# Where a stick-breaking attention and HGRN2 kernel builds its masks, splits its value weights, and lays its first diagonal

## The chip, the cores and the metric

The kernel runs on one core of one Trainium2 chip. The metric is the device time of one execution in microseconds (us); less is better. The engines are named as the profile names them: PE is TensorE (matmuls), DVE is VectorE, ACT is ScalarE, POOL is GpSimd, and SP is the queue from which most loads are issued.

## The reference: what is computed

One layer of a streaming encoder, for one sequence of 1024 tokens of width 1024, in float32:

```python
xn = rmsnorm(x, norm1_g);  u = xn @ w_in
q_sb, k_sb, v_sb, f_raw, i_hg, q_hg, g_hg, gate_sb, gate_hg = split(u)

# 8 heads of 64: strictly causal stick-breaking attention
z = q_sb . k_sb / 8
w = sigmoid(z_ts) * prod over s<j<t of (1 - sigmoid(z_tj));   o_sb = w @ v_sb

# 4 heads of 128: HGRN2 recurrence in chunks
lb = cumsum(softmax(lb_logits));  f = lb + (1 - lb) * sigmoid(f_raw);  k = 1 - f
S_t = diag(f_t) S_(t-1) + k_t v_t^T;   o_t = S_t^T silu(q_hg)_t        # v = i_hg
o_hg = rmsnorm(o_hg) * silu(g_hg)

merged = sigmoid(gate_sb + b) * (o_sb @ w_o_sb) + sigmoid(gate_hg + b) * (o_hg @ w_o_hg)
h = x + merged @ w_out
h = h + relu(rmsnorm(h) @ w_ff1)^2 @ w_ff2;   out = rmsnorm(h, final_g)
```

## The kernel before

**Products.** Every float32 matrix is split into a high and a low half: ACT copies it to the high half (`hi_copy`, L151), DVE subtracts that from the source and writes the low half (`lo_sub`, L156); `hi_lo` (L159) does both. A product is then three matmuls per tile (high by high, high by low, low by high), recorded at L128. A plain product on DVE (`mul`) is recorded at L164. So a matmul that reads a low half waits for DVE, and DVE for ACT.

**Stages, in time.** Norm of x and transposes (to 35 us), the attention heads (35 to 310), the recurrence, head by head (310 to 560), then gates, output product, second norm and MLP. In the attention each item is one head and one block of 128 queries: `scores` (L741) computes z on PE and its sigmoids on ACT, `weights` (L772) runs the reversed product as a scan on DVE (L782) and multiplies (bt by rm, L164), `turn` (L796) transposes the weights on PE (pw, L131) and splits them (wTh, wTl), and `values` (L838) multiplies them with V (po) and adds two halves into osb (L858), which the last one stores (od, by POOL).

**The recurrence.** `hg_levels(h)` (L976) makes the decayed score matrix sc of one head (1024 columns, 8 chunks of 128) from k, q and the decay pp. The diagonal is a sum over channels of k times q: `pairs_of("sd...")` makes the products (sd_x), splits them (sd_h, sd_l), and `sums_of` lets PE sum them with a matrix of ones (sd). Level l then covers blocks of 2 to the l: level 0 and 1 also by such sums (sl_x, sl_h, sl_l, products on DVE, sums on PE), levels 2 to 6 by direct matmuls of k and q (`scores_of`). At each level `mul` folds the decay into k, q and pp for half of the columns at a time; results are laid into sc under masks (`lay`, L1021, and L1077), the diagonal by a product with the identity. The masks are bit patterns of 128 by 128 that `make_masks` (L942) computes from two iotas on POOL and seventeen small operations on DVE; nothing reads them before the recurrence.

**What sets the order.** The program is recorded in one order and a scheduler lays out each engine's queue, which the engine runs strictly in order. `after(a, b)` (L105) makes a stand behind b in the order without a wait. PE's matmuls belong to two lanes: "main" blocks (attention, recurrence) and "fill" steps of a stream of projections `st`; a fill block may run up to AHEAD = 2 main blocks early. `st.advance(n, upto)` issues n fill steps between main blocks; the loop over heads (FILL, L2202 and on) hands out a fixed share of steps to each level. In the stretch concerned the fill is first the projection of head 1's query and gate (pjq, pjg: matmuls of 128x512), then the values of the recurrence for all heads (pji, weights wi).

**Weights of the fill.** `Unit.load` brings raw weights (512 KB each) into one of two buffers tagged "raw" (pool `wts`, bufs=2) and `Unit.split` makes high and low halves. A load waits until the buffer's last reader, normally the low half's subtraction, is done, and the loads of one queue go in order. `Stream._start` splits the unit that begins, and `prefetch` splits the next unit and loads the one behind it. wi is wide: four raw pieces (wir), four splits (wih on ACT, wil on DVE), all recorded at its prefetch.

Of the kernel before, what the change touches and what calls it, by code (L numbers as in the profile page):

```python
# [14 lines left out]
ALU = mybir.AluOpType  # L15
# [10 lines left out]
HGW = 512  # L26
# [13 lines left out]
def kernel(  # L40
# [178 lines left out]
    oml = cpool.tile([P, 4], F32, tag="oml", name="oml")  # L219
    lmx = small.tile([P, 4], F32, tag="lmx", name="lmx")  # L220
    le = small.tile([P, 8], F32, tag="le", name="le")
    def lower_bounds():
        nc.vector.tensor_tensor(
            out=lmx, in0=prm[:, LB0 : LB0 + 4], in1=prm[:, LB1 : LB1 + 4], op=ALU.max
        )
        for j in range(2):
            nc.vector.tensor_tensor(
                out=le[:, 4 * j : 4 * j + 4],
                in0=prm[:, LB0 + 4 * j : LB0 + 4 * j + 4],
                in1=lmx,  # L230
                op=ALU.subtract,
            )
        nc.scalar.activation(le, le, AF.Exp)
        nc.vector.tensor_tensor(out=lmx, in0=le[:, 0:4], in1=le[:, 4:8], op=ALU.add)
        nc.vector.reciprocal(lmx, lmx)
        mul(lb, le[:, 0:4], lmx)
        nc.vector.tensor_scalar(
            out=oml, in0=lb, scalar1=-1.0, scalar2=1.0, op0=ALU.mult, op1=ALU.add
        )

# [531 lines left out]
    def weights(h, qb):  # L772

        nk = (qb + 1) * P
        bt, rm = zs[h, qb]
        cut = qb == NT - 1
        parts = ((512, nk - 1), (0, 512)) if cut else ((0, nk - 1),)
        for i, (a, b) in enumerate(parts):  # L780
            rr = rm[:, a:b][:, ::-1]
            sc = nc.vector.tensor_tensor_scan(  # L782
                out=rr,
                data0=rr,
                data1=bits[:, 1024 - nk + a : 1024 - nk + b][:, ::-1],
                initial=rm[:, b : b + 1] if i else 0.0,
                op0=ALU.mult,
                op1=ALU.max,
            )
            if i == 1 or (qb == 5 and h in (2,)):  # L790
                after(sc, turn_lo[0])
            m = mul(bt[:, a:b], bt[:, a:b], rm[:, a:b])
            if qb == 5:
                after(m, turn_lo[0])
# [83 lines left out]
    def f_epilogue(h):  # L878
# [15 lines left out]

        return ep

    def i_job():
        unit = wide_unit("wi", W_IN, C_I, HGW)

        vs = []  # L900

        def ep(ps, tb):
            for h in range(NHG):
                if tb == 0:
                    vs.append(slot(f"v{h}"))
                    hg[h, "v"] = vs[h]
                nc.scalar.copy(vs[h][:, tb * P : (tb + 1) * P], ps[:, h * P : (h + 1) * P])
            if tb == NT - 1:
                vs.clear()

        return st.add([unit], lambda: token_steps("pji", unit, xn, range(NT), ep, n=HGW))
# [30 lines left out]
    def make_masks():  # L942
        mscr = slot_n("mscr", 4 * P, I32)
        mask_bits = hpool.tile([P, 4 * 512], U8, tag="h", name="masks")
        m_x, m_s, m_gt, m_odd = (mscr[:, i * P : (i + 1) * P] for i in range(4))
        nc.gpsimd.iota(m_x, pattern=[[1, P]], base=0, channel_multiplier=0)
        nc.gpsimd.iota(m_s, pattern=[[0, P]], base=0, channel_multiplier=1)
        nc.vector.tensor_tensor(out=m_gt, in0=m_x, in1=m_s, op=ALU.is_gt)
        nc.vector.tensor_scalar(out=m_odd, in0=m_s, scalar1=1, scalar2=None, op0=ALU.bitwise_and)
        nc.vector.tensor_tensor(out=m_x, in0=m_x, in1=m_s, op=ALU.bitwise_xor)  # L950

        def add_mask(l, m_if):
            nc.vector.tensor_scalar(
                out=m_s, in0=m_x, scalar1=l, scalar2=None, op0=ALU.logical_shift_right
            )
            m = mask_bits[:, len(masks) * P : (len(masks) + 1) * P]
            nc.vector.scalar_tensor_tensor(
                out=m, in0=m_s, scalar=1.0, in1=m_if, op0=ALU.is_equal, op1=ALU.mult
            )
            masks.append(m)  # L960

        for l in (0, *range(2, 5)):
            add_mask(l, m_gt)

        mul(m_odd, m_odd, m_gt)
        add_mask(1, m_odd)
        nc.vector.tensor_tensor(out=m_odd, in0=m_gt, in1=m_odd, op=ALU.subtract)
        add_mask(1, m_odd)
# [7 lines left out]
    def hg_levels(h):  # L976
# [17 lines left out]
        def pairs_of(name, n, *products):  # L994

            t, h_, l_ = (slot_n(f"{name}_{x}", n, d) for x, d in zip("xhl", (F32, F32R, F32R)))
            for (a, b, w), (i, cs) in zip(products, halves()):
                mul(t[:, cs].rearrange("p (n c) -> p n c", c=w) if w else t[:, 0:n], a, b)
            after(hi_lo(h_, l_, t), turn_lo[0] if "sd0" in name else None)
            return name, n, h_, l_  # L1000

        def sums_of(pairs):

            name, n, h_, l_ = pairs
            open_block("main")
            banks = []
            for c0 in range(0, n, 512):
                S = bank(f"{name}_{c0}")
                matmul(S, ones, h_[:, c0 : c0 + 512], start=True, stop=False)
                matmul(S, ones, l_[:, c0 : c0 + 512], start=False, stop=True)  # L1010
                banks.append(S)
            return banks
# [4 lines left out]
        def lay(mask, S, H):  # L1017

            right = sc.rearrange("p (c n two h) -> p c n two h", c=NT, two=2, h=H)[:, :, :, 1]
            m = blocks_of(mask, H)[:, :, 1].unsqueeze(1).to_broadcast([P, NT, P // (2 * H), H])  # L1020
            nc.vector.copy_predicated(  # L1021
                right, m, S.rearrange("p (c n h) -> p c n h", c=NT, h=H)
            )

        pairs = pairs_of(f"sd{h}", T, (k, q, 0))
        for _, cs in halves():
            mul(q[:, cs], q[:, cs], dec[:, cs])
        yield
        for l in range(7):
            H = 1 << l  # L1030
# [4 lines left out]
            if l == 0:  # L1035
                pairs = pairs_of(
                    f"sl{h}_{l}", 512, (blocks_of(k, 1)[:, :, 0, 0], blocks_of(q, 1)[:, :, 1, 0], 0)
                )
            elif l == 1:
                kv, qv = blocks_of(k, 2)[:, :, 0], blocks_of(q, 2)[:, :, 1]  # L1040
                pairs = pairs_of(
                    f"sl{h}_{l}",
                    T,
                    *((kv[:, :, i : i + 1].to_broadcast([P, T // 4, 2]), qv, 2) for i in (1, 0)),
                )
            elif l < 5:
                banks = scores_of(f"sl{h}_{l}")
            else:
                open_block("main")
                S = bank(f"sl{h}_{l}")  # L1050
                for i, s0 in enumerate(c * P + b for c in range(NT) for b in blocks):
                    matmul(
                        S[0:H, i * H : (i + 1) * H],
                        k[:, s0 : s0 + H],
                        q[:, s0 + H : s0 + 2 * H],
                        start=True,
                        stop=True,
                    )
# [4 lines left out]
                mul(qv[:, :, 1, :], qv[:, :, 1, :], left.to_broadcast([P, n, H]))  # L1063
                hg_level[0] = mul(right, right, left)
            if l == 0:
                for i, cs in halves():
                    mul(chunks(sc[:, cs]), chunks(sums[i]), over_chunks(ident))
            elif l == 1:
                lay(masks[0], sums[0], 1)
            elif l == 2:  # L1070
                for m, S in zip(masks[-2:], sums):
                    lay(m, S, 2)
# [1084 lines left out]
    turns["on"] = False  # L2157
    turn_vectors(1, 6)
    lower_bounds()
    st.advance(11, j_qk[0])  # L2160
    scores(*items[0])
    weights(*items[0])
    st.advance(1, j_qk[0])
    scores(*items[1])
    make_masks()
    st.finish(j_qk[0])

    n_fill = 9 * (j_q[1] - j_qk[0]) + 9
# [4 lines left out]
    for i, it in enumerate(items):  # L2173
        if i + 1 < len(items):
            weights(*items[i + 1])
        if i + 2 < len(items):
            st.finish(j_qk[items[min(i + 4, len(items) - 1)][0]])
            scores(*items[i + 2])
        if i % 2 == 1:
            next(wsums, None)  # L2180
        want = n_first + (i + 1) * (n_fill - n_first) // len(items)
        st.advance(want - done, j_q[1])
        done = want
        before = ready.popleft() if ready else None

        def between():
            if before:
                values(*before)

        r = turn(*it, between)  # L2190
        if i == len(items) - 2:
            attended[0] = turn_lo[0]
        if it[1] != NT - 1:
            between()
        if r:
            ready.append(r)
    while ready:
        values(*ready.popleft())
    st.finish(j_q[1])


    FILL = (3.75, 3.3, 2.7, 2.5, 2.9)  # L2202
# [120 lines left out]
```

## Time and profile before

| | us |
|---|---|
| time, median of 3 runs | 1444.68 (1444.64 to 1444.85) |
| the profiled execution | 1444.55 |
| its span, first to last instruction | 1442.8 |
| PE busy | 1430.3 (99%) |
| DVE busy | 1105.2 (77%) |
| ACT busy | 665.4 (46%) |
| POOL busy | 141.0 (10%) |
| mean granted TensorE clock | 0.999 of full speed |

A row of the timeline reads: start and duration in us, engine, line, operation, destination from sources, shapes, number of instructions in the row; in brackets the idle time of the engine before it and what released it. Instructions of one engine overlap a little, as the next starts before the last has ended, so distances between starts say more than durations. A row of the waits reads: engine, what it was about to write and the line, what it waited for, then us in total, how often, and the longest. A row of stretches reads: from and to, length, then busy us and instructions of PE, PE's weight loads, DVE, ACT and POOL, the granted clock, the share of the DMA engines and their GB/s. A row of one tile reads: line, engine, operation, count, then duration in ns (least, median, most) and first and last start in us; and the landing times of its transfers from issue.

### The profile page before, as it was taken

The page shows a single profiled execution, that of the slowest core. Times are in us where ns is not written, and L with a number is a line of the kernel's source. Part 1 is how long each engine was busy: PE and PEld are TensorE (multiplying, and loading weights), DVE is VectorE, ACT ScalarE, POOL GpSimd, SP SyncE. Part 2 cuts the span into 40 slices and gives each one's busy share as a digit, 9 for nine tenths or more (in the row PEclk, how much of TensorE's full clock was granted, in tenths as well). Part 3 has the DMA queues.
Part 4 walks back from the last instruction along what each step waited for, and adds up shares of the span by engine and source line. Part 5 has one row for each costly group of instructions (what it writes and reads, how often), then busy time and mean ns, then how long its engine had stood idle before and what let it go on. Part 6 is the DMA issues. An engine that isn't in the chain of part 4 may idle for free.

```text
span 1442.8 us, 19614 instructions
## 1 busy us (share of the span) xinstructions
PE 1430.3 (99%) x7272; PEld 1209.7 (84%) x7272; DVE 1105.2 (77%) x1583; ACT 665.4 (46%) x1151; POOL 141.0 (10%) x338
## 2 busy tenths in 40 slices
PE   9999999999999999999999999999999999999998
PEld 8889988888888888888888888888888888888886
DVE  7799898988367798788787898666666757768765
ACT  7566666652223244432335574444444433523343
POOL 3121122200000012100000300000000000000042
PEclk9999999999999999999999999999999999999999
DMA  7135154341113349755487415344445974776825
GB/s 213 48 92 130 32 108 76 73 99 42 52 45 102 88 153 254 240 178 171 142 298 250 155 50 182 130 143 159 155 151 206 354 262 170 261 276 233 288 100 184
DMA packets 157751, 228.85 MB, mean 159 GB/s; under 512 B 25772, under 2 KB 91864, under 8 KB 157656
## 3 DMA queue, kind: packets, MB, share of 16 engines
q1 hardware_dynamic: 142680, 186.96, 38.5%
q0 software_dynamic: 11520, 34.61, 9.2%
q10 hardware_dynamic: 3456, 6.03, 1.1%
q8 instruction: 57, 0.93, 0.3%
q14 instruction: 38, 0.31, 0.1%
HBM read 164.12 MB, written 63.44 MB: 158 GB/s over the span
## 4 chain that ended last, share of the span: by engine, by line
PE 94%; DVE 2%; ACT 1%; issue 1%; DMA 1%; POOL 1%; SPq 0%; DVEq 0%; ACTq 0%; POOLq 0%
PE pm L128 21%; PE pX L128 9%; PE pW L128 6%; PE pY L128 6%; PE pjqk L128 5%; PE pga L128 3%; PE pjq L128 3%; PE pjf L128 3%; PE pys L128 3%; PE pyh L128 3%; PE gY L128 3%; PE gX L128 3%; PE pji L128 3%; PE po L128 3%; PE sl L128 2%; PE pjg L128 2%
## 5 line engine op out<-in xcount | busy, mean ns | idle before, releaser
L151 ACT CAST whid<-w 128x1024 fp32r<-128x1024 f32 x30 | 31.6, 1054 | 154.1 <-PE pm L128 89.4
L782 DVE TENSOR_TENSOR_SCAN rm<-rm,bits 128x511 f32<-128x511 f32 (+7 forms) x72 | 87.3, 1219 | 13.5 <-ACT rm L760 13.4
L128 PE MATMUL pm<-wlod,sh 128*128 128x512 f32 x240 | 93.5, 389 | 0.0
L128 PE MATMUL pm<-whid,sl 128*128 128x512 f32 x240 | 93.4, 389 | 0.0
L128 PE MATMUL pm<-whid,sh 128*128 128x512 f32 x240 | 93.4, 389 | 0.0
L128 PE MATMUL pm<-tl,sh 128*128 128x512 f32 (+1 forms) x210 | 81.3, 387 | 0.0
L128 PE MATMUL pm<-th,sl 128*128 128x512 f32 (+1 forms) x210 | 81.3, 387 | 0.0
L128 PE MATMUL pm<-th,sh 128*128 128x512 f32 (+1 forms) x210 | 81.3, 387 | 0.0
L156 DVE TENSOR_TENSOR wlod<-w,whid 128x1024 fp32r<-128x1024 f32 x30 | 36.6, 1221 | 55.2 <-ACT whid L151 55.2
L156 DVE TENSOR_TENSOR sl<-sa,sh 128x1024 fp32r<-128x1024 f32 x56 | 68.2, 1217 | 0.3 <-ACT sh L151 0.3
L151 ACT CAST wTh<-pw 128x512 fp32r<-128x512 f32 (+2 forms) x96 | 44.0, 486 | 51.3 <-PE pw L131 50.7
L151 ACT CAST sh<-sa 128x1024 fp32r<-128x1024 f32 x56 | 57.2, 1046 | 7.4 <-DMA sa<-ad 7.4
L1963 POOL TENSOR_SCALAR fss<-fss 128x1 f32<-128x1 f32 x8 | 4.5, 561 | 562.1 <-ACT fsc L1958 561.6
L128 PEld LDWEIGHTS pm<-wlod,sh 128*128 128x128 f32 x240 | 45.0, 188 | 9.8 <-DVE wlod L156 0.4
L128 PEld LDWEIGHTS pm<-whid,sl 128*128 128x128 f32 x240 | 45.1, 188 | 9.3
L128 PEld LDWEIGHTS pm<-whid,sh 128*128 128x128 f32 x240 | 45.0, 187 | 9.3
L156 DVE TENSOR_TENSOR wTl<-pw,wTh 128x512 fp32r<-128x512 f32 (+2 forms) x96 | 50.6, 547 | 2.8 <-ACT wTh L151 2.1
L164 DVE TENSOR_TENSOR bt<-bt,rm 128x511 f32<-128x511 f32 (+7 forms) x72 | 49.0, 685 | 3.6
L128 PE MATMUL pX<-sql,t1h 128*128 128x512 f32 x128 | 50.0, 391 | 0.1
L128 PE MATMUL pX<-sqh,t1l 128*128 128x512 f32 x128 | 49.8, 389 | 0.0
L128 PE MATMUL pX<-sqh,t1h 128*128 128x512 f32 x128 | 49.8, 389 | 0.0
L760 ACT ACTIVATE rm<-z 128x511 f32<-128x511 f32 (+4 forms) x96 | 48.1, 502 | 3.1 <-PE z L128 1.2
(921 smaller groups left out, 4520.8 us busy)
## 6 DMA issues: line engine op xcount, KB each, us to landing
w<-in_w_ff_dram SPq DMA_DIRECT2D x72, 512.0 KB, 5.1
sa<-ad SPq DMA_DIRECT2D x56, 512.0 KB, 6.8
ad<-a SPq DMA_DIRECT2D x32, 256.0 KB, 2.1
ad<-s SPq DMA_DIRECT2D x16, 512.0 KB, 5.8
tw<-in_w_out_dram POOLq DMA_DIRECT2D x24, 256.0 KB, 3.9
x<-in_x_dram SPq DMA_DIRECT2D x8, 512.0 KB, 8.6
xnl<-xnh POOLq DMA_DIRECT2D x8, 512.0 KB, 11.0
pr<-pd SPq DMA_DIRECT2D x8, 512.0 KB, 6.4
```

Source lines behind the costliest of these rows:

```text
L128: return pe(nc.tensor.matmul(*a, **k))
L151: hi_last[0] = after(in_turn("act", nc.scalar.copy(dst, src)), hi_behind[0])
L156: nc.vector.tensor_tensor(out=dst, in0=src, in1=hi.bitcast(F32), op=ALU.subtract),
L164: return nc.vector.tensor_tensor(out=out, in0=a, in1=b, op=ALU.mult)
L760: nc.scalar.activation(rm[:, s0 + c0 - 1 : s0 + m - 1], z[:, c0:m], AF.Sigmoid, scale=-0.125)
L782: sc = nc.vector.tensor_tensor_scan(out=rr, data0=rr, data1=bits[:, 1024 - nk + a : 1024 - nk + b][:, ::-1], initial=rm[:, b : b + 1] if i ...
L1963: nc.gpsimd.tensor_scalar(out=ssq, in0=ssq, scalar1=1.0 / D, scalar2=EPS, op0=ALU.mult, op1=ALU.add)
```

## The change

Four things change; the numbers of instructions stay.

1. `make_masks()` is called right after `lower_bounds()` instead of after the second `scores`. Its first two DVE operations stand behind the last of `lower_bounds` (`bounded`, L237), and the scan of the first attention item stands behind the last mask (`masked`).
2. The unit wi becomes a `ByParts` unit: the prefetch only records the loads of the four raw pieces; the four splits are recorded one at a time in `hg_levels(0)`: after the first products q by decay, after level 0's products, and ahead of and behind level 1's.
3. In `pairs_of` the order "behind the last attention weights' split" for head 0's diagonal (`turn_lo`) moves from the split to the product sd_x. The products q by decay stand behind sd_x. The diagonal of head 0 is laid one level later, behind the products of level 1 (`pairs[4]`), and the copy of level 0's sums stands behind the remainder sl_l of level 1 (`pairs[5]`).
4. One fill step is issued ahead of the last `values`, and `st.finish(j_q[1])` moves in front of them.

```diff
--- before.py
+++ after.py
@@ -219,6 +219,8 @@
     oml = cpool.tile([P, 4], F32, tag="oml", name="oml")
     lmx = small.tile([P, 4], F32, tag="lmx", name="lmx")
     le = small.tile([P, 8], F32, tag="le", name="le")
+    bounded, masked = [None], [None]
+
     def lower_bounds():
         nc.vector.tensor_tensor(
             out=lmx, in0=prm[:, LB0 : LB0 + 4], in1=prm[:, LB1 : LB1 + 4], op=ALU.max
@@ -234,7 +236,7 @@
         nc.vector.tensor_tensor(out=lmx, in0=le[:, 0:4], in1=le[:, 4:8], op=ALU.add)
         nc.vector.reciprocal(lmx, lmx)
         mul(lb, le[:, 0:4], lmx)
-        nc.vector.tensor_scalar(
+        bounded[0] = nc.vector.tensor_scalar(
             out=oml, in0=lb, scalar1=-1.0, scalar2=1.0, op0=ALU.mult, op1=ALU.add
         )
 
@@ -787,6 +789,8 @@
                 op0=ALU.mult,
                 op1=ALU.max,
             )
+            if (h, qb) == items[0]:
+                after(sc, masked[0])
             if i == 1 or (qb == 5 and h in (2,)):
                 after(sc, turn_lo[0])
             m = mul(bt[:, a:b], bt[:, a:b], rm[:, a:b])
@@ -894,8 +898,19 @@
 
         return ep
 
+    class ByParts(Unit):
+        def split(self, upto=None):
+            self.load()
+            if self.hl is None:
+                self.hl = []
+            else:
+                Unit.split(self, upto)
+
+    u_i = wide_unit("wi", W_IN, C_I, HGW)
+    u_i.__class__ = ByParts
+
     def i_job():
-        unit = wide_unit("wi", W_IN, C_I, HGW)
+        unit = u_i
 
         vs = []
 
@@ -945,8 +960,8 @@
         m_x, m_s, m_gt, m_odd = (mscr[:, i * P : (i + 1) * P] for i in range(4))
         nc.gpsimd.iota(m_x, pattern=[[1, P]], base=0, channel_multiplier=0)
         nc.gpsimd.iota(m_s, pattern=[[0, P]], base=0, channel_multiplier=1)
-        nc.vector.tensor_tensor(out=m_gt, in0=m_x, in1=m_s, op=ALU.is_gt)
-        nc.vector.tensor_scalar(out=m_odd, in0=m_s, scalar1=1, scalar2=None, op0=ALU.bitwise_and)
+        after(nc.vector.tensor_tensor(out=m_gt, in0=m_x, in1=m_s, op=ALU.is_gt), bounded[0])
+        after(nc.vector.tensor_scalar(out=m_odd, in0=m_s, scalar1=1, scalar2=None, op0=ALU.bitwise_and), bounded[0])
         nc.vector.tensor_tensor(out=m_x, in0=m_x, in1=m_s, op=ALU.bitwise_xor)
 
         def add_mask(l, m_if):
@@ -954,10 +969,11 @@
                 out=m_s, in0=m_x, scalar1=l, scalar2=None, op0=ALU.logical_shift_right
             )
             m = mask_bits[:, len(masks) * P : (len(masks) + 1) * P]
-            nc.vector.scalar_tensor_tensor(
+            made = nc.vector.scalar_tensor_tensor(
                 out=m, in0=m_s, scalar=1.0, in1=m_if, op0=ALU.is_equal, op1=ALU.mult
             )
             masks.append(m)
+            masked[0] = made
 
         for l in (0, *range(2, 5)):
             add_mask(l, m_gt)
@@ -995,13 +1011,13 @@
 
             t, h_, l_ = (slot_n(f"{name}_{x}", n, d) for x, d in zip("xhl", (F32, F32R, F32R)))
             for (a, b, w), (i, cs) in zip(products, halves()):
-                mul(t[:, cs].rearrange("p (n c) -> p n c", c=w) if w else t[:, 0:n], a, b)
-            after(hi_lo(h_, l_, t), turn_lo[0] if "sd0" in name else None)
-            return name, n, h_, l_
+                x = mul(t[:, cs].rearrange("p (n c) -> p n c", c=w) if w else t[:, 0:n], a, b)
+                after(x, turn_lo[0] if "sd0" in name else None)
+            return name, n, h_, l_, x, hi_lo(h_, l_, t)
 
         def sums_of(pairs):
 
-            name, n, h_, l_ = pairs
+            name, n, h_, l_ = pairs[:4]
             open_block("main")
             banks = []
             for c0 in range(0, n, 512):
@@ -1018,13 +1034,19 @@
 
             right = sc.rearrange("p (c n two h) -> p c n two h", c=NT, two=2, h=H)[:, :, :, 1]
             m = blocks_of(mask, H)[:, :, 1].unsqueeze(1).to_broadcast([P, NT, P // (2 * H), H])
-            nc.vector.copy_predicated(
+            return nc.vector.copy_predicated(
                 right, m, S.rearrange("p (c n h) -> p c n h", c=NT, h=H)
             )
+
+        def diagonal(sums, behind=None):
+            for i, cs in halves():
+                after(mul(chunks(sc[:, cs]), chunks(sums[i]), over_chunks(ident)), behind)
 
         pairs = pairs_of(f"sd{h}", T, (k, q, 0))
         for _, cs in halves():
-            mul(q[:, cs], q[:, cs], dec[:, cs])
+            after(mul(q[:, cs], q[:, cs], dec[:, cs]), pairs[4])
+        if h == 0:
+            u_i.split(1)
         yield
         for l in range(7):
             H = 1 << l
@@ -1036,13 +1058,19 @@
                 pairs = pairs_of(
                     f"sl{h}_{l}", 512, (blocks_of(k, 1)[:, :, 0, 0], blocks_of(q, 1)[:, :, 1, 0], 0)
                 )
+                if h == 0:
+                    u_i.split(2)
             elif l == 1:
+                if h == 0:
+                    u_i.split(3)
                 kv, qv = blocks_of(k, 2)[:, :, 0], blocks_of(q, 2)[:, :, 1]
                 pairs = pairs_of(
                     f"sl{h}_{l}",
                     T,
                     *((kv[:, :, i : i + 1].to_broadcast([P, T // 4, 2]), qv, 2) for i in (1, 0)),
                 )
+                if h == 0:
+                    u_i.split()
             elif l < 5:
                 banks = scores_of(f"sl{h}_{l}")
             else:
@@ -1063,10 +1091,14 @@
                 mul(qv[:, :, 1, :], qv[:, :, 1, :], left.to_broadcast([P, n, H]))
                 hg_level[0] = mul(right, right, left)
             if l == 0:
-                for i, cs in halves():
-                    mul(chunks(sc[:, cs]), chunks(sums[i]), over_chunks(ident))
+                if h > 0:
+                    diagonal(sums)
+                else:
+                    first_sums = sums
             elif l == 1:
-                lay(masks[0], sums[0], 1)
+                if h == 0:
+                    diagonal(first_sums, pairs[4])
+                after(lay(masks[0], sums[0], 1), pairs[5] if h == 0 else None)
             elif l == 2:
                 for m, S in zip(masks[-2:], sums):
                     lay(m, S, 2)
@@ -2157,12 +2189,12 @@
     turns["on"] = False
     turn_vectors(1, 6)
     lower_bounds()
+    make_masks()
     st.advance(11, j_qk[0])
     scores(*items[0])
     weights(*items[0])
     st.advance(1, j_qk[0])
     scores(*items[1])
-    make_masks()
     st.finish(j_qk[0])
 
     n_fill = 9 * (j_q[1] - j_qk[0]) + 9
@@ -2194,9 +2226,10 @@
             between()
         if r:
             ready.append(r)
+    st.finish(j_q[1])
+    st.advance(1, j_hg[1])
     while ready:
         values(*ready.popleft())
-    st.finish(j_q[1])
 
 
     FILL = (3.75, 3.3, 2.7, 2.5, 2.9)
```

In the queues that the scheduler makes of it, PE runs four of the six matmuls of that fill step (pjg) between the first and second po of the last values, and one fill step more stands ahead of each main block of head 0; from head 1's diagonal on, the order on PE is as before. DVE's order differs in the two stretches concerned, and the two iotas on POOL come behind the memset of ones at the start. The order of the loads on SP is unchanged.

## The prediction

> **What bounds the kernel now.** I read the busy shares first, then TensorE's waits, then the instructions around each wait.
>
> ```profile
> PE 1430.3 (99%) x7272; PEld 1209.7 (84%) x7272; DVE 1105.2 (77%) x1583; ACT 665.4 (46%) x1151; POOL 141.0 (10%) x338
> ```
>
> TensorE (PE) is busy for 1430.3 of the 1442.8 us span. The change adds and removes no matmul, so all it can win is time in which PE waits.
>
> ```profile
> engine line waited for: us in total, times, longest us
> PE warm L128 <- POOL ident masks.py:199: 2.2, 1, 2.2
> PE po L128 <- DVE wTl L156: 1.5, 2, 1.0
> PE sl L128 <- DVE sl_l L156: 1.0, 1, 1.0
> ```
>
> The 2.2 us is the start of the program, before anything can be multiplied, and stays. The two po waits and the sl wait are the prize. Each is for the low half of a split (L156), which VectorE (DVE) makes.
>
> ```profile
> 68.22 0.36 PE L128 MATMUL po<-wTh,V 128*128 128x256 f32 x1
> 69.61 0.39 PE L128 MATMUL po<-wTl,V 128*128 128x256 f32 x1 [1.02 <-DVE wTl L156]
> 69.83 0.28 PE L128 MATMUL po<-wTh,V 128*128 128x256 f32 x1
> 69.95 0.29 PE L128 MATMUL po<-wTl,V 128*128 128x256 f32 x1
> ...
> 309.45 0.38 PE L128 MATMUL po<-wTh,V 128*128 128x256 f32 x1 [0.18 <-ACT wTh L151]
> 310.30 0.39 PE L128 MATMUL po<-wTl,V 128*128 128x256 f32 x1 [0.47 <-DVE wTl L156]
> 310.52 0.28 PE L128 MATMUL po<-wTh,V 128*128 128x256 f32 x1
> ...
> 327.66 0.39 PE L128 MATMUL sl<-sl_h,ones 128*128 128x512 f32 x1
> 329.06 0.50 PE L128 MATMUL sl<-sl_l,ones 128*128 128x512 f32 x1 [1.01 <-DVE sl_l L156]
> 329.40 0.40 PE L128 MATMUL sl<-sl_h,ones 128*128 128x512 f32 x1
> ...
> 329.87 1.95 PE L128 MATMUL sl<-q,k 128*128 128x128 f32 x16
> 331.57 0.48 PE L128 MATMUL pji<-wih,xnh 128*128 128x512 f32 x1
> ```
>
> The bracketed idle time starts at a matmul's modelled end, so I measure the loss from start to start. Undisturbed po matmuls start 0.12 us apart (69.83 to 69.95), wide ones 0.23–0.24 (two from 329.40 to 329.87). First place: 69.61 − 68.22 − 0.12 = 1.27 us, and the next start comes 0.22 instead of 0.12 later: 1.37. Second: 310.30 − 309.45 − 0.12 = 0.73, plus 0.10: 0.83. Third: 329.06 − 327.66 − 0.23 = 1.17, plus 0.34 − 0.23 = 0.11: 1.28. Together **3.48 us**. That is the ceiling, and about 0.24% of the time.
>
> **The change part by part.**
>
> *Masks behind the lower bounds.* What makes wTl late at the first place:
>
> ```profile
> 67.03 0.28 DVE L957 SCALAR_TENSOR_TENSOR masks<-mscr 128x128 uint8<-128x128 int32 x1
> 67.23 1.74 DVE L782 TENSOR_TENSOR_SCAN rm<-rm,bits 128x767 f32<-128x767 f32 x1
> 68.90 1.12 DVE L156 TENSOR_TENSOR wTl<-pw,wTh 128x512 fp32r<-128x512 f32 x2
> L957 DVE SCALAR_TENSOR_TENSOR masks<-mscr 128x128 uint8<-128x128 int32 x6 | 1.6, 270 | 0.0
> L953 DVE TENSOR_SCALAR mscr<-mscr 128x128 int32<-128x128 int32 x6 | 1.3, 219 | 0.0
> 66.55 0.96 ACT L151 CAST wTh<-pw 128x512 fp32r<-128x512 f32 x2
> ```
>
> Twelve of the mask operations, six of L957 and six of L953, are 2.9 us busy between 56.5 and 67.3, and five more are like them; as the next instruction can start some 0.2 us after such a one (67.03 to 67.23), less after the short L953, all seventeen cost DVE about 3 us. All stand ahead of the 1.74 us scan, and the scan ahead of wTl. Without them the scan ends about 3 us earlier, near 65.9. ScalarE's (ACT) wTh then decides: its two pieces take 0.48 each from 66.55, so the first wTl runs from about 67.1 to 67.8. PE wants it at 68.22 + 0.12 = 68.34: 0.5 us to spare. The whole 1.37 goes.
>
> The masks move here:
>
> ```profile
> 38.98 0.17 DVE L237 TENSOR_SCALAR oml<-lb 128x4 f32<-128x4 f32 x1
> 41.51 0.69 DVE L156 TENSOR_TENSOR KS<-pjqk,KS 64x512 fp32r<-64x512 f32 x1 [2.36 <-ACT QH L151]
> ```
>
> DVE is idle for 2.36 us behind oml, and the scheduler lays twelve of the mask operations ahead of KS and five among its followers. If they run over, KS and QL slip by up to 0.7 us (3 less 2.36); what they feed, a transfer of QL and then z, is not among PE's waits today, so it has some room that I can't size from a row. Price 0, at worst 0.7. The two POOL iotas (0.27 us each) go behind the memset of ones, where POOL next waits for x; price 0.
>
> *One fill step ahead of the last values.* One step of six pjg matmuls now comes before head 0's recurrence, and four of the six are issued between the first and the second po of the second place. 4 × 0.23 = 0.9 us of work that was due anyway stands where PE lost 0.73, so the 0.83 goes. The 0.18 us on wTh in front stays. Their weights were split long before:
>
> ```profile
> L156 DVE TENSOR_TENSOR wg1l<-wg1r,wg1h x1: 1199/1199/1199, 292.7 to 292.7; 128x1024 fp32r<-128x1024 f32 x1
> ```
>
>  The price is passed on: every main block of head 0 now has one fill step more in front, and the next block needing DVE is met later by PE, which helps.
>
> *Value weights one by one, remainders first.* The third place:
>
> ```profile
> 313.33 2.56 SPq L136 DMA_DIRECT2D wir<-in_w_in_dram  x2
> 314.50 0.58 POOL L867 DMA_DIRECT2D od<-osb  x1 [13.10 <-DVE osb L858]
> 321.70 1.23 DVE L156 TENSOR_TENSOR wil<-wir,wih 128x1024 fp32r<-128x1024 f32 x1 [1.59 <-ACT wih L151]
> 322.96 1.29 DVE L164 TENSOR_TENSOR sc<-sd,ident 128x512 f32<-128x512 f32 x2
> 324.16 0.68 DVE L164 TENSOR_TENSOR g<-pjg,g 128x512 f32<-128x512 f32 x1
> 324.76 1.28 DVE L164 TENSOR_TENSOR sl_x<-k,q 128x512 f32<-128x512 f32 x2
> 325.96 1.32 DVE L1021 COPY_PREDICATED sc<-masks,sl 128x512 f32<-128x512 uint8 x1
> 327.78 1.22 DVE L156 TENSOR_TENSOR sl_l<-sl_x,sl_h 128x1024 fp32r<-128x1024 f32 x1
> DMA to landing us min/median/max: 3.7/4.4/5.0
> ```
>
> DVE stood 1.59 us at the fourth wil, whose raw weights were issued at 315.5 (the second of two SP issues that end at 315.89) and took 5.0; behind it came the diagonal (sc, 1.2 us), g, the products sl_x, the copy of the level-0 sums (1.1 us) and two small ones, then sl_l. In the new order DVE does sd_x, osb, q, osb, sd_l, wil, sl_x, wil, sl_l, six small k/q/pp steps, g, and then the third wil, which I call S. Adding start-to-start distances (1.13 for a 1024 split or product, 0.6 for 512, 0.33 for k or q) from the wTl at 309.56, with the second osb waiting for the last po until about 314.1, puts its earliest start at S = 321.9. Then come sl_x (1.2), five small steps (1.67) and sl_l (1.13): the remainder is ready at S + 5.25 = 327.2. PE reaches sl_1 at 327.66 − 0.83 (second place) + 6 × 0.227 (one fill step more in front) = 328.2 and its sl_l at 328.4. Over 1 us to spare; the 1.28 goes. The 18 pji matmuls in front of it start at 324.1, and the third wil, for the last six, is needed at 326.8 and done at 323.1.
>
> What is late next: the work that was put back. It fills a DVE already full:
>
> ```profile
> 321.70:342.80 21.10, 20.09 (x105) 16.88 (x105) 21.07 (x38) 6.17 (x14) 0.00 (x0) 1.00 0.31 89
> ...
> 331.91 1.22 DVE L1187 TENSOR_TENSOR wga0r<-wga0r,wga0r 128x1024 f32<-128x1024 f32 x1
> 335.45 0.42 DVE L164 TENSOR_TENSOR q<-q,pp 128x256 f32<-128x256 f32 x1
> 342.34 0.42 DVE L164 TENSOR_TENSOR q<-q,pp 128x256 f32<-128x256 f32 x1
> ```
>
> DVE (the third pair of numbers) is busy 21.07 of 21.10 us from the fourth wil to the last q that level 4 needs, which ends at 342.76, 21.06 after that wil. The new order has in that stretch one wil more (+1.14), one g less (−0.60) and one q of head 1 less (−0.64): 20.96 from S, so 342.9 for S = 321.9. PE goes from 328.2 through sl_1 (0.9), level 2 (329.87 to 331.57: 1.7), 24 pji (5.45), level 3 (1.7) and 18 pji (4.1) to level 4's first half at about 342.2 and its second 0.85 later, at 343.05; q for the first half is ready at S + 20.2 = 342.1. For level 3 the last q (335.45 + 0.42 is 14.17 behind the old wil) is ready at S + 14.7 = 336.6, against 337.2. So level 4 has 0.1–0.2 us to spare, level 3 0.5. The subtraction on wga0r stands at S + 10.75 = 332.6; its load can only be issued when the fourth wil frees the raw buffer, about S + 6.45 = 328.4, and took
>
> ```profile
> DMA to landing us min/median/max: 4.5/4.5/4.5
> ```
>
> so it lands near 332.9, 0.2 late. I put 0.2 us for these against the sum. Any delay of S beyond 321.9 comes out at PE nearly one for one.
>
> What can delay S is the third raw load. Two buffers serve four loads, and now it waits for the first wil (315.6 to 316.9) instead of being issued at 313.33. Landing plus ACT's wih (1.05) must come by 321.9, so it may take 4.0 us. Of the rows 3.7, 4.4 and 5.0, I take 3.7: the 5.0 load was issued 1.0 us behind the 512 KB od store (314.50) and while the load before it was in flight; in the new order no other load is, and the store, issued with the last osb near 314.6, is 2.3 us ahead. With 4.4, S is 0.5 later and the sum 2.8; with 5.0, 1.1 later and 2.2. The Trainium skill ("DMA: Bandwidth & Descriptors", "Anatomy of one DMA — SWDGE (gpsimd) path") gives about 2.0 us fixed plus bytes at 436 GB/s: for 512 KB an estimate of 3.2 us, by which S would not move and the sum stay as it is. This trace's rows are 0.5 to 1.8 us above that, and they decide.
>
> **Sum.** 1.37 + 0.83 + 1.28 − 0.2 = 3.3 us. The profiled execution took 1444.55 (span 1442.77 and 1.8 around it), the median of the runs is 1444.68, 0.13 more: 1444.68 − 3.3 = **1441.4 us**. What a measurement of this kernel tells from no change is about 0.2%, or 2.89 us; faster means below 1441.79.
>
> **The rivals.**
>
> *The wait moves to levels 3 and 4.* The third wir takes 4.4 to 5.0 or DVE loses as much elsewhere. For it: DVE has no idle time there to absorb anything. Against: the slower load shared its time with the store. The gain is 2.2 to 2.8 (1441.9 to 1442.5), centre 1442.2, inside 0.2%.
>
> *One place isn't cured.* If wTl stays behind some other work at the first place, 1.37 stays: 1442.7. If sl_l does (an ACT cast of wih ahead of sl_h), 1.28 stays: 1442.6. Against: margins of 0.5 and 1.2 us. The masks could also push QL into the next z; that would cost at most 0.7.
>
> *Slower: the raw loads run late.* The one serial chain that became longer is wil, buffer free, load, wih, wil, buffer free, wga0r load. At 3.7 us it costs nothing; beyond 4.0 each us costs one, the gain of 3.3 is used up at 4.0 + 3.3 = 7.3 us, and slower by over 0.2% needs 10.2. The rows reach 5.0 here; a load of 7.5 gives 1444.9. A wait of more than 3.4 us would by the Trainium skill ("TensorE: Matmul & The Clock Gate", "What's actually happening") also halve the clock for a while; the granted clock around today's waits of 1.0 us is 1.00, and no run here shows more.
>
> **How the numbers follow.** Forecast 0.62; the wait moves 0.20; one place isn't cured 0.10; slower chain 0.08, most of it for what I haven't seen in a schedule this dense. Only the forecast is faster by over 0.2%, and close to the bound; the middle cases give 0.31 within 0.2%, as does a little of the last; 0.07 slower. The low end is the ceiling, 1444.68 − 3.48, less 0.2 for the spread: 1441.0. The high end takes in the moved wait and the uncured places, 1442.9; this leaves out about one in ten. The forecast's own range is 1441.0 to 1441.8.
>
> **What would show it.** PE's waits keep no po on wTl above 0.1 us and no sl on sl_l; the scan of 767 starts near 64.2; DVE runs masks from 39.2. At 320 to 330 (all later times shifted by about 1.4 us earlier) DVE starts its third wil without a wait on ACT. Wrong would be: a new PE wait at sl<-q,k near 335 to 342 (the chain of waits then names DVE q, before it wga0r or wih and a DMA), po still waiting near 68, or loads of wir above 4.0 us.

## The result, and the profile after

The changed kernel takes 1441.95 us (median of 14 runs, 1441.26 to 1442.30) against 1444.68 (14 runs, 1444.31 to 1445.03): 2.73 us less, a ratio of 0.998 with a 95% interval of 0.9972 to 0.9988. The forecast was 1441.4 with a range of 1441.0 to 1442.9. The gain is real, though just under the 0.2% (2.89 us) that the chances were drawn by; the median lies with the first rival (1441.9 to 1442.5), where the wait moves to level 4.

The profiled execution took 1442.05 with a span of 1440.2, 2.6 less than before. Its waits of TensorE, columns as before:

```profile
PE warm L128 <- POOL ident masks.py:199: 2.2, 1, 2.2
PE pjqk L128 <- DVE xnl L334: 0.3, 1, 0.3
PE po L128 <- ACT wTh L151: 0.2, 1, 0.2
PE pjv L128 <- ACT wv0h L151: 0.2, 1, 0.2
PE sl L128 <- DVE q L164: 0.2, 1, 0.2
```

The two po waits on wTl and the sl wait on sl_l are gone. Two small ones are new: pjv near 14 us, and sl on q, which is level 4 of head 0. PE at the three places, and at level 4 (timeline of the changed kernel):

```profile
68.65 0.36 PE L128 MATMUL po<-wTh,V 128*128 128x256 f32 x1
68.85 0.28 PE L128 MATMUL po<-wTl,V 128*128 128x256 f32 x1
...
308.59 0.39 PE L128 MATMUL po<-wTh,V 128*128 128x256 f32 x1 [0.18 <-ACT wTh L151]
308.81 0.40 PE L128 MATMUL pjg<-xnh,wg1h 128*128 128x512 f32 x1
...
309.51 0.40 PE L128 MATMUL pjg<-xnh,wg1h 128*128 128x512 f32 x1
309.75 0.27 PE L128 MATMUL po<-wTl,V 128*128 128x256 f32 x1
...
327.44 0.39 PE L128 MATMUL sl<-sl_h,ones 128*128 128x512 f32 x1
327.67 0.39 PE L128 MATMUL sl<-sl_l,ones 128*128 128x512 f32 x1
...
341.90 1.27 PE L128 MATMUL sl<-q,k 128*128 128x128 f32 x9 [0.16 <-DVE q L164]
```

At the first place the po on wTl now follows the one on wTh by 0.20 instead of 1.39; at the second, four pjg stand between them; at the third, sl_l follows sl_h at the undisturbed 0.23. At level 4 the first matmul starts 0.32 late and the next one 0.11 more: 0.43 us lost.

DVE in the stretch of the masks and at the third wil:

```profile
39.37 0.17 DVE L239 TENSOR_SCALAR oml<-lb 128x4 f32<-128x4 f32 x1
39.45 0.28 DVE L963 TENSOR_TENSOR mscr<-mscr 128x128 int32<-128x128 int32 x1
...
42.54 0.69 DVE L156 TENSOR_TENSOR KS<-pjqk,KS 64x512 fp32r<-64x512 f32 x1
...
64.75 1.74 DVE L784 TENSOR_TENSOR_SCAN rm<-rm,bits 128x767 f32<-128x767 f32 x1
67.58 1.15 DVE L156 TENSOR_TENSOR wTl<-pw,wTh 128x512 fp32r<-128x512 f32 x2 [1.09 <-ACT wTh L151]
...
321.66 1.23 DVE L156 TENSOR_TENSOR wil<-wir,wih 128x1024 fp32r<-128x1024 f32 x1 [0.36 <-ACT wih L151]
...
342.22 0.42 DVE L164 TENSOR_TENSOR q<-q,pp 128x256 f32<-128x256 f32 x1
```

The scan of 767 runs 2.5 us earlier, although this profile is 0.4 us late at this point, and wTl now waits for ACT. The third wil waited 0.36 for ACT's wih. Whether that wait is what comes out at level 4 is tested below. ACT and SP show where it comes from:

```profile
316.26 2.11 SPq L136 DMA_DIRECT2D wir<-in_w_in_dram  x2
320.57 1.05 ACT L151 CAST wih<-wir 128x1024 fp32r<-128x1024 f32 x1 [2.54 <-DMA wir<-in_w_in_dram]
```

The load was issued at 316.26 and used at 320.57: 4.3 us, 4.2 of them to its landing, where the forecast had 4.0 as the limit.

### The profile page after: what moved, and what is told of

Same layout as the page of the kernel before. It is cut to its first block, busy times and chain, and to the rows that moved or that the text cites. A ratio compares the mean times of both kernels' runs of the same rounds, so it can differ in the third digit from the quotient of the medians.

```text
span 1440.2 us, 19612 instructions
## 1 busy us (share of the span) xinstructions
PE 1430.0 (99%) x7272; PEld 1210.0 (84%) x7272; DVE 1106.4 (77%) x1583; ACT 665.7 (46%) x1151; POOL 137.8 (10%) x338
## 4 chain that ended last, share of the span: by engine, by line
PE 95%; DVE 2%; DMA 1%; issue 1%; POOL 1%; ACT 1%; SPq 0%; DVEq 0%; POOLq 0%; ACTq 0%
PE pm L128 21%; PE pX L128 9%; PE pW L128 6%; PE pY L128 6%; PE pjqk L128 6%; PE pga L128 3%; PE pjq L128 3%; PE pjf L128 3%; PE pys L128 3%; PE pyh L128 3%; PE gY L128 3%; PE gX L128 3%; PE po L128 3%; PE z L128 2%; PE pjv L128 2%; PE pjg L128 2%
```

## The experiments

The runs come in three groups of four, each measured beside the kernel before. That took 1444.70 in the first group (the load early, head 1's sd_x late, both, the iotas late), 1444.63 in the second (the load early with the gate's split kept, the masks alone, wi split whole, the old order of the diagonal) and 1445.07 in the third (the fill step alone, the masks undone, and two repeats). As these differ by 0.44, a difference of less than half a us between groups says little by itself.

**The wait at level 4: the load, or DVE's amount of work?** Two edits of the changed kernel relieve either.

```diff
+    u_i.roomy = (2,)       # the third raw piece of wi gets a slot of its own
```

> The changed kernel with the third raw piece of wi loaded into a slot of its own, so that it waits for no split. The changed kernel took 1441.95 (median), with DVE idle for 0.36 us at the third wil and PE losing 0.43 us at level 4 of head 0 (start to start). Theory: the late load put those 0.36 us into a full DVE queue, and they came out at level 4. Then the wait at the third wil goes, the loss at level 4 falls by 0.36 or all of it, and the time is about 1441.55 (1441.4 to 1441.7). Rival: DVE's amount of work alone makes level 4 late; then the loss at level 4 stays above 0.3 and the time at 1441.9 to 1442.0.

1441.91 (1441.77 to 1442.55): no gain. The wait at the third wil and the loss at level 4 were gone, but PE's waits had a new line, and the timeline shows where:

```profile
PE sl L128 <- DVE sc L164: 0.5, 1, 0.5
327.97 1.05 PE L128 MATMUL sl<-q,k 128*128 128x128 f32 x8
329.51 1.16 PE L128 MATMUL sl<-q,k 128*128 128x128 f32 x8 [0.48 <-DVE sc L164]
...
323.38 1.23 DVE L156 TENSOR_TENSOR wga0wlo<-wga0r,wga0whi 128x1024 fp32r<-128x1024 f32 x1
...
328.76 1.29 DVE L164 TENSOR_TENSOR sc<-sd,ident 128x512 f32<-128x512 f32 x2
```

With the load early, the scheduler had also moved the split of the gate's weights (wga0wlo) ahead of sl_l, from 331 to 323. That pushed the diagonal (sc) back, and the second half of level 2 waits for it (sl behind sc: the diagonal still holds the PSUM bank). Level 2's sixteen matmuls took 2.45 us from first start to next instead of 1.70: 0.75 us lost. So neither theory was tested cleanly; what it did show is that laying the diagonal one level later leaves its banks little to spare.

```diff
@@ pairs_of
-                after(x, turn_lo[0] if "sd0" in name else None)
+                after(x, turn_lo[0] if "sd0" in name else level3[0] if "sd1" in name else None)
@@ behind the k, q, pp steps of level 3
+            if h == 0 and l == 3:
+                level3[0] = hg_level[0]
```

> The changed kernel with head 1's products sd_x (one DVE instruction, 1.2 us) put behind the k, q and pp steps that level 4 of head 0 needs. Theory (a full DVE queue sets level 4): the loss of 0.43 us at level 4 goes though the load stays late and the wait at the third wil stays 0.3 to 0.4; time about 1441.5. Rival: the moved product is late for its own sums on PE (head 1's sd) and the loss comes back there; 1441.9 or more.

1441.38 (1440.96 to 1441.86), with no loss at level 4. That is the time the theory gave. Its other half, a wait of 0.3 to 0.4 us at the third wil, did not come: the third load happened to land earlier, and its wil started at 321.01, 0.65 earlier than in the changed kernel's profile, after an idle time of 0.05. So this run doesn't decide.

```diff
@@ both edits
+    u_i.roomy = (2,)
+                after(x, turn_lo[0] if "sd0" in name else level3[0] if "sd1" in name else None)
```

> The third raw piece of wi early and head 1's sd_x late, together. If both act on the same loss at level 4 (0.43 us), the two together give what each gives alone, about 1441.5, with no loss above 0.1 at level 4. If they act on different losses, more: 1441.1.

1442.00 (1441.44 to 1442.57): the moved gate split was there again and PE lost 0.67 at level 2, so this says the same as the first run.

To take the load alone, the gate's split was tied back to its place:

```diff
+    u_i.roomy = (2,)
@@ RawUnit.split, first gate unit
-            hi_lo(h, l, ra)
+            lo = hi_lo(h, l, ra)
+            if self.name == "wga0":
+                after(lo, laid0[0])     # behind the copy of level 0's sums
```

> The changed kernel with the third raw piece of wi in a slot of its own, as in the run before, but with the split of the gate's weights (wga0) kept behind the copy of level 0's sums, so that DVE's order is that of the changed kernel. In the run before, this split had moved ahead of sl_l, and PE lost 0.65 us at level 2, where a PSUM bank is held by the diagonal's product sc. Theory: in the old order both losses are gone, at level 2 and at level 4: 1441.45 (1441.3 to 1441.7), the third wil starts without a wait. Rival: the early load itself does the harm; 1441.9.

1441.34 (1441.13 to 1441.98). The loss at level 2 and the late start of level 4 are gone, with the wil at

```profile
321.11 1.22 DVE L156 TENSOR_TENSOR wil<-wir,wih 128x1024 fp32r<-128x1024 f32 x1
```

and no wait; 0.10 us stays behind the first matmul of level 4. The changed kernel was not in this group, but of its 25 runs elsewhere 11 took more than 1442.0, and of these 11 none. The profiles in which DVE's order in this stretch is the changed kernel's and the load is late say the same (us):

| profile | third load, issue to landing | DVE idle before the third wil | lost at level 4 |
|---|---|---|---|
| changed kernel | 4.2 | 0.36 | 0.43 |
| iotas late | 4.0 | 0.15 | 0.33 |
| masks undone | 4.0 | 0.11 | 0.32 |
| changed kernel, second profile | 3.8 | 0 | 0.12 |

So both theories hold a part: about 0.1 us is lost even when DVE doesn't wait, as its queue is full, and the rest goes with the late load. When the load isn't late, the forecast's figure of 1441.4 is reached.

**Is the start late because of the iotas?**

```diff
-        nc.gpsimd.iota(m_x, pattern=[[1, P]], base=0, channel_multiplier=0)
-        nc.gpsimd.iota(m_s, pattern=[[0, P]], base=0, channel_multiplier=1)
+        after(nc.gpsimd.iota(m_x, ...), last_power[0])
+        after(nc.gpsimd.iota(m_s, ...), last_power[0])
```

> The changed kernel with the two iotas on POOL behind the norms' last power, instead of behind the memset of ones at 2.3 us. In the profiles the changed kernel's PE is 0.37 us later than the kernel before at 18 us, because the second raw value weight landed later (ACT waits for it until 13.28). Theory A: this is chance in the first loads, not the iotas: time 1441.95 within 0.2, runs spread from 1441.3 to 1442.3 as in the changed kernel. Theory B: the iotas disturb the first loads: the start is as before, time about 1441.55, and the runs lie close together.

1441.71 (1441.32 to 1441.93), between the two theories. But the run with the early third load and the changed kernel's own second profile have the iotas in the same early place, and there PE starts pjv 0.34 and 0.17 us earlier than in the first profile, without that wait. So the iotas don't make it late by themselves; that it is chance in the first loads is the reading left, which no run shows, and the runs' spread isn't settled by it.

**The parts alone.**

```diff
@@ the kernel before, with the masks' move alone (and the two orders that hold them there)
+    make_masks()            # behind lower_bounds()
-    make_masks()            # behind the second scores
```

> The kernel before with the masks' move alone (order behind the lower bounds, first scan behind the last mask). Theory: the wait of po on wTl near 69 goes and nothing else changes: 1444.68 - 1.37 = 1443.3, and the waits near 310 and 329 stay at 0.5 and 1.0 us. Rival: DVE's time in front (12 masks ahead of KS) is paid at z; 1443.6 or more.

1443.94 (1443.10 to 1444.33): 0.7 us, half of what was expected. The profile is of the slowest of these runs. Near 69 the loss is gone, and PE is 1.25 us ahead. But:

```profile
PE sl L128 <- DVE sl_l L156: 1.3, 1, 1.3
PE po L128 <- DVE wTl L156: 0.5, 1, 0.5
PE sl L128 <- DVE q L164: 0.4, 1, 0.4
...
311.97 2.55 SPq L136 DMA_DIRECT2D wir<-in_w_in_dram  x2
320.83 1.23 DVE L156 TENSOR_TENSOR wil<-wir,wih 128x1024 fp32r<-128x1024 f32 x1 [1.84 <-ACT wih L151]
```

the wait for sl_l grew from 1.0 to 1.3 (1.56 instead of 1.17 from start to start), because ACT could cast the last raw piece only 0.87 us earlier than before (319.75 instead of 320.62), and the end of head 3's levels near 556 took 0.66 us longer. In this profile other places gave most of the gain back; how much they do in a median run is not shown. Undoing the masks from the changed kernel gives the other side:

```diff
@@ the changed kernel, with the masks as before
-    make_masks()            # behind lower_bounds()
+    make_masks()            # behind the second scores
```

> The changed kernel with the masks built where they were. Alone, the masks' move gave 0.7 instead of 1.37, as the wait for sl_l grew by 0.4 and loads near 555 were late in its profile. Theory: place by place the masks are worth 1.37 us: 1441.9 + 1.37 = 1443.3. Rival: they are worth 0.7: 1442.6.

1443.07 (1442.77 to 1443.85) against 1441.90 of the changed kernel in the same group: the masks are worth 1.17, with 1.26 us lost again at po near 69.6. Where the later waits are out of the way, the masks bring nearly what the first place lost.

```diff
@@ the kernel before, with the fill step alone
+    st.finish(j_q[1])
+    st.advance(1, j_hg[1])
     while ready:
         values(*ready.popleft())
-    st.finish(j_q[1])
```

> The kernel before with the fill step ahead of the last values alone. The step begins the unit whose prefetch splits wi, so all four wil are recorded, and laid by the scheduler, ahead of sd_x. Theory: the loss of 0.83 us near 310 goes and about 6 us come at head 0's diagonal, with the TensorE clock lower for some us behind so long a wait, as without the splitting by parts (1449.4): 1450 (1448.5 to 1452). Rival: the step alone gives its 0.8: 1443.9.

1450.94 (1450.58 to 1451.43), 5.9 us slower than before. And the changed kernel without the splitting by parts:

```diff
-    u_i.__class__ = ByParts
```

> The changed kernel with wi split whole at its prefetch, all else as changed. The prefetch is recorded at the fill step, which now lies ahead of the last values, so that all four wil stand ahead of sd_x on DVE, two of them behind loads that wait for buffers. Theory: sd_x comes near 321 and sd_l near 323.5 to 324, where PE wants it at 317.5; PE loses about 6 us: 1448 (1446 to 1450), slower than before. Rival: the splits one by one are a refinement worth the 1.28 us at level 1 at most; 1442 to 1443.3.

1449.37 (1447.80 to 1450.68). In both, head 0's diagonal waits 5.9 us. PE and DVE of the second:

```profile
315.94 0.39 PE L128 MATMUL pjg<-xnh,wg1l 128*128 128x512 f32 x1
322.26 1.22 PE L128 MATMUL sd<-sd_h,ones 128*128 128x512 f32 x2 [5.93 <-ACT sd_h L151]
...
309.71 2.35 DVE L156 TENSOR_TENSOR wil<-wir,wih 128x1024 fp32r<-128x1024 f32 x2
312.09 0.99 DVE L862 TENSOR_TENSOR osb<-po,ot 64x256 f32<-64x256 f32 x2
315.91 1.23 DVE L156 TENSOR_TENSOR wil<-wir,wih 128x1024 fp32r<-128x1024 f32 x1 [2.83 <-ACT wih L151]
318.71 1.23 DVE L156 TENSOR_TENSOR wil<-wir,wih 128x1024 fp32r<-128x1024 f32 x1 [1.58 <-ACT wih L151]
319.85 1.22 DVE L164 TENSOR_TENSOR sd_x<-k,q 128x1024 f32<-128x1024 f32 x1
322.31 1.22 DVE L156 TENSOR_TENSOR sd_l<-sd_x,sd_h 128x1024 fp32r<-128x1024 f32 x1
```

The fill step begins its unit, and with it the prefetch: the four splits of wi come ahead of sd_x in DVE's queue, the last two waiting 2.83 and 1.58 us for loads. So the splitting by parts is first of all what makes the fill step possible.

The loss is larger than the wait. Stretches of the same profile, columns as before, and two of its matmuls:

```profile
310.00:316.00 6.00, 6.00 (x35) 5.17 (x34) 3.01 (x5) 1.78 (x3) 0.58 (x1) 1.00 0.59 191
322.00:328.00 6.00, 5.74 (x13) 4.30 (x14) 5.97 (x13) 2.27 (x4) 0.00 (x0) 0.50 0.20 58
328.60:334.00 5.40, 5.40 (x25) 4.41 (x25) 5.40 (x11) 1.65 (x2) 0.00 (x0) 1.00 0.00 0
327.17 0.63 PE L128 MATMUL pjg<-xnl,wg1h 128*128 128x512 f32 x1
327.59 0.63 PE L128 MATMUL pjg<-xnh,wg1l 128*128 128x512 f32 x1
```

Behind the wait the granted clock is 0.50 for some 6 us, and matmuls start 0.42 apart instead of 0.23; of the 9.1 us lost from 316 to 328.4, 6.1 are the wait and 3.0 the clock. That agrees with what the Trainium skill says ("TensorE: Matmul & The Clock Gate", "What's actually happening"), that an idle window of about 3.4 us puts TensorE to half its clock. In the run with the fill step alone less was enough: the clock fell 2.4 us after the last matmul's end (317.7 to 320.2), and the measurement decides. The waits of 1.0 us before the change lay in stretches with a clock of 1.00.

The run with the fill step alone waited as long (5.87 us) and lost less. The clock is 0.50 for some 6.8 us in both profiles, but with the fill step alone from 320.2 to 327.0, and without the splitting by parts from 321.5 to 328.4. The first stretch lies half within the wait: only 3.4 us of it were left when PE went on, and 1.7 us were lost to it instead of 3.0. So the price of such a wait depends also on when the clock falls.

The splitting by parts alone, and the changed kernel without the fill step, were not run; what these two are worth is read from the profile.

**Is the new order of the diagonal needed?** The changed kernel without its third part:

```diff
-                after(x, turn_lo[0] if "sd0" in name else None)
-            return name, n, h_, l_, x, hi_lo(h_, l_, t)
+            return name, n, h_, l_, x, after(hi_lo(h_, l_, t), turn_lo[0] if "sd0" in name else None)
-            after(mul(q[:, cs], q[:, cs], dec[:, cs]), pairs[4])
+            mul(q[:, cs], q[:, cs], dec[:, cs])
-                if h > 0:
-                    diagonal(sums)
-                else:
-                    first_sums = sums
+                diagonal(sums)
-                if h == 0:
-                    diagonal(first_sums, pairs[4])
-                after(lay(masks[0], sums[0], 1), pairs[5] if h == 0 else None)
+                lay(masks[0], sums[0], 1)
```

> The changed kernel without its third part: sd_x, q by decay, the diagonal and level 0's copy in the order of the kernel before; masks, wi by parts and the fill step stay. Theory 1 (the splits in front of sl_l were what made it late): DVE reaches the third wil near 320.6, its load having been issued early (the first wil again comes ahead of osb), sl_l is in time, level 4 too; 1441.4, so the new diagonal order earns nothing or costs 0.5. Theory 2 (the diagonal and the copy, 2.3 us together, were what made it late): PE waits about 1.1 us for sl_l at level 1; 1443.0.

1441.28 (1440.64 to 1443.00), with no loss at levels 1 to 4. The slowest run is the one profiled, and its loss lies elsewhere:

```profile
PE pkv L128 <- ACT pp L1124: 1.4, 1, 1.4
560.78 1.05 ACT L151 CAST wo01h<-wo01r 128x1024 fp32r<-128x1024 f32 x1 [5.12 <-DMA wo01r<-in_w_o_sb_dram]
```

A load of output weights, issued at 547.04, was used at 560.78, and the copy of pp behind it on ACT made PE wait. In the run with the early load and the kept order, the same cast began at 558.09 and PE lost nothing. As that left a doubt, both kernels ran again, together.

> The changed kernel once more, beside the runs below on the same chip: 1441.9 (1441.3 to 1442.3), with a loss of 0.2 to 0.5 us at level 4 of head 0 in the profile.

> The changed kernel without its third part, once more: one profile of it fell on a late load of output weights near 555, and the median stood 0.67 below the changed kernel's. Theory 1 (the new diagonal order is not needed and costs what level 4 loses): 1441.3, 0.4 to 0.7 below the changed kernel of this call, no loss at levels 1 and 4. Theory 2 (the difference was chance in the loads): equal within 0.2.

1441.90 (1441.29 to 1442.23) for the changed kernel, 1441.53 (1440.98 to 1442.79) without the third part: 0.37 lower side by side. (The 0.67 of the expectation compares two groups.) The runs overlap, so that the version without it is faster isn't shown; nothing speaks for its being slower. DVE without the third part:

```profile
312.87 0.43 DVE L862 TENSOR_TENSOR osb<-po,ot 64x256 f32<-64x256 f32 x1 [0.21 <-ACT ot L861]
313.33 0.69 DVE L164 TENSOR_TENSOR sl_x<-k,q 128x512 f32<-128x512 f32 x1
...
317.81 1.29 DVE L164 TENSOR_TENSOR sc<-sd,ident 128x512 f32<-128x512 f32 x2
319.01 0.68 DVE L164 TENSOR_TENSOR g<-pjg,g 128x512 f32<-128x512 f32 x1
319.61 1.22 DVE L156 TENSOR_TENSOR wil<-wir,wih 128x1024 fp32r<-128x1024 f32 x1
```

The first wil stands ahead of osb again, so the third load is issued at 312.23, and the third wil starts at 319.61 without a wait, though the diagonal is laid ahead of it.

The changed kernel's second profile is its own experiment. Its execution took 1441.29, level 4 starts in time, and its load shows the difference:

```profile
316.09 2.11 SPq L136 DMA_DIRECT2D wir<-in_w_in_dram  x2
319.99 1.05 ACT L151 CAST wih<-wir 128x1024 fp32r<-128x1024 f32 x1 [2.12 <-DMA wir<-in_w_in_dram]
321.08 1.23 DVE L156 TENSOR_TENSOR wil<-wir,wih 128x1024 fp32r<-128x1024 f32 x1
341.30 1.94 PE L128 MATMUL sl<-q,k 128*128 128x128 f32 x15
```

3.9 us from issue to use, and no wait at the wil; in the first profile 4.3, and 0.36. Same program, same order: 0.4 us in a landing make 0.3 us at level 4 (0.43 against 0.12).

## Why the prediction was right, and where it was off

- *The masks.* Right: wTl then waits for ACT's wTh and PE for nothing. 1.37 was forecast. From the first po on wTh to the next one, 1.61 us became 0.32, so 1.29 were won: the undisturbed distance at this place is 0.20, and not the 0.12 of later po that the sum took. Undone from the changed kernel the masks are worth 1.17, alone 0.7. The overrun into KS was allowed for (KS starts at 42.54 instead of 41.51, about 0.4 of it from the late start) and cost nothing at z.
- *The fill step.* The wait went as forecast, four pjg in between. From the first po on wTh to the next, 1.07 us became 0.33 (1.27 less 0.94 for the pjg): 0.74 won, where 0.83 was forecast for the same reason as above. The sentence that the step's price "is passed on" and "helps" missed what the step also does: it begins a unit and so records the prefetch earlier. Alone, this costs 5.9 us. The forecast stood because the second part catches it, and it didn't say so; for this part that was luck.
- *The third place.* Right in time: sl_l was in place, and 1.29 were won, where 1.28 was forecast. Its explanation, that the diagonal and the copy had to get out of the way, is not needed: with wi split by parts, the old order of the diagonal is in time as well, and a little better for the load.
- *What is late next.* Right in place and mechanism: DVE is full from the third wil to level 4, and a late third load comes out there nearly one for one. The term was mis-sized: the sum put 0.2 us for it, and it was 0.43 in one profile of the changed kernel and 0.12 in the other. The step that failed is "Of the rows 3.7, 4.4 and 5.0, I take 3.7": from issue to landing it was 4.2 in the one and 3.8 in the other, on either side of the stated 4.0. Its reason, that no other load would be in flight, did not hold, as the fourth raw load was issued at 318.0, 2.5 us before the third landed; whether that slowed the third is not shown. The room of 0.1–0.2 us at level 4 wasn't there either, as 0.1 is lost without a late load.
- *The number.* With the load early and the order kept, the kernel is at 1441.34, the forecast's 1441.4; the changed kernel itself, at 1441.95, is above the forecast's own 1441.8 and inside the stated range only because that takes in the rivals. Two of the forecast's own signs of being wrong came in the first profile, a PE wait at sl<-q,k (341.90) and a load of wir above 4.0 us (4.2); in the second neither did. So what the forecast called the first rival is what some executions do and others don't.
- *The estimate for the load.* The 3.2 us that the prediction works out from the Trainium skill ("DMA: Bandwidth & Descriptors", "Anatomy of one DMA — SWDGE (gpsimd) path") go by a fit for transfers that POOL issues. These loads are issued by SP, and the third and fourth of wi took 3.6 to 5.5 us in the profiles here.
- *Not in the sum.* The profiled execution was 0.37 us late by 18 us, from the first loads, and lost 0.11 us within level 3 beside the 0.43 at level 4. With the three places this makes −1.29 − 0.74 − 1.29 + 0.11 + 0.43 + 0.37 = −2.41; behind head 0's levels PE is 2.34 earlier than before (372.21 against 374.55), at its last matmul 2.54, and the span is 2.6 shorter, so some 0.2 of the gain lie further on and stay unassigned. What makes the changed kernel's runs spread over 1.0 us (1441.26 to 1442.30) is shown for single profiles (the first loads, the third wir, loads near 555), not for the runs as a whole.
- *The slower rival.* It did not come. The nearest to it is the kernel without the splitting by parts: there the loads and splits of wi do hold PE up, but because all four splits stand in front of sd_x, and not because a load took beyond 7.3 us; the longest of them took 5.5.

## What to carry to other kernels

When a wait is removed by filling an in-order engine's idle time, walk its queue on to the next place at which another engine reads from it, with the landing times of the loads as a range: a margin under half a microsecond is decided by the loads from run to run. A step of background work that is moved forward brings what it sets off with it (here the next unit's splits), and this can cost more than the wait it covers. Before several reorderings are kept together, take each out of the whole: here one of them was as fast left out.

## What the runs showed that was not expected

A wait of TensorE for 5.9 us cost 9.1 in one run and 7.7 in another, as the granted clock stood at 0.50 for 6.8 us in both and more or less of that fell behind the wait. One load of 512 KB, otherwise harmless, took 13.7 us from issue to use in one execution (547.04 to 560.78), which cost 1.7 us. And a single changed load (the third raw piece in a slot of its own) let the scheduler move another split 8 us forward, which cost about as much as the load gained.
